# A two-layer hybrid block: the recurrent branch's projection, three pairs inside the recurrent part and one pair behind it

## The chip, the cores and the metric

The kernel runs on one core of a Trainium2 chip. The metric is the device time of one launch in microseconds (us). Three runs of the kernel before took 3108.33, 3111.07 and 3115.43 us; their median is 3111.07 us. About 0.2% (6.2 us) is what a measurement of this kernel can tell from no change.

## The reference, cut to what matters

The program is a block of two layers. Each layer is a feed-forward net, a mixer of three branches (attention, the recurrent branch RWKV7, the state-space branch S5) and a second feed-forward net. Layer 0 works on 512 tokens (256 of the sequence and 256 of the context), layer 1 on the 256 of the sequence.

```python
def gated_merge(z_gate, ya, yr, ys, branch_proj, w_out):
    ga, gr, gs = jnp.split(jax.nn.sigmoid(z_gate), N_BRANCH, axis=-1)
    m = ga * (ya @ branch_proj[0]) + gr * (yr @ branch_proj[1]) + gs * (ys @ branch_proj[2])
    return m @ w_out
```

`yr` is 512 wide: eight heads of 64, that is four pairs of heads of 128. `yr @ branch_proj[1]` is a sum over those four pairs, each of 128 rows of the 512x1024 weight. Ahead of it stands, pair by pair, the branch's `finish`: group normalisation of the scan's output, a bonus term and a gate.

## The kernel before, in words

All activations lie feature-major: a tile has 128 features as partitions and the tokens (512 or 256) as columns. Products of float32 are made as three products of split operands (`mm3`, L153, L154, L155): an operand is a high part (a cast) and a low part (what the cast left out). The split of a weight is a load on SP's queue (L135), a cast on ACT (L136, `wh`) and a subtraction (L137, `wl`) on DVE, or on every second weight on POOL while `k.aside` is set. A weight whose split is made with the priority `AHEAD` stands earlier in the engines' queues than its place in the code. The split of an activation (`split_slot`) is a cast on ACT (L1016) and a subtraction on POOL (L1017).

In the mixer the branches for attention and S5 and the gates' products come first. Then comes what is called the recurrent part here: `conduct` (L980) runs the four pairs' chains of chunks, the last step of each pair being `finish` (L905 to L929), and a filler, the generator `project` (L1645). A stream yields how long it thinks that its step takes, or the name of something that it waits for; `conduct` takes up the first stream whose time has come. In this part PE executes in the order in which the code is written down (`manual_schedule`); the other engines are ordered by a scheduler's priorities. PE's accumulators `acc` have two buffers there, the gates' tiles `sg` two.

`project` makes branch 0 (attention) and branch 2 (S5) with `Merge.branch` (L1573): for each of eight output blocks f of 128 features, a weight of 256 KB, a gate read back from DRAM on ACT's queue (L1584), four times three products into `acc`, and sg = gate * acc on DVE (L1594); for branch 2, m[f] += sg on POOL (L1595).

`finish` of a pair: PE L913 (mean), DVE L917, ACT L918 (square), PE L920 (gate), then a power of the variance (PE L181, DVE L183, POOL L184, ACT L186, PE L190), DVE L923 to L926, and on SP a write of the pair's result to `rwy` in DRAM (L927).

Behind the recurrent part, branch 1 (the recurrent one) is made in the same way: four readbacks of `rwy` (L1570), the splits, eight f with twelve products each, all of this before `m` is split into `mp` (L1690, L1691) and goes through `w_out` in `down` (L381): products L397, L398, L399, the first half of the output's columns streamed weight by weight, the second half kept as eight weights and gone through token tile by token tile.

Of the kernel before, what the change touches and what calls it, by code (L numbers as in the profile page):

```python
# [12 lines left out]
ALU = mybir.AluOpType  # L13
# [11 lines left out]
P = 128  # L25
HIGH = 300
WB, NWA = (3, 3, 3), 2
HELD, NFIRST, AHEAD = 8, 5, 600
# [4 lines left out]
class Ctx:  # L33
# [57 lines left out]
    def late(self, base, tag="late", bufs=12):  # L91
        return self.sp.tile([P, 512], F32, name=self.n(base), tag=tag, bufs=bufs)
# [238 lines left out]
def first_sums(k, w, cols, u, nstream, then):  # L331

    k.more_weights(None, None, None)
    sums = [k.acc() for _ in cols]
    for c, ps in zip(cols, sums):
        k.sum(ps[:, :256], k.columns(w, c, ahead=AHEAD), [(h[:, :256], l[:, :256]) for h, l in zip(*u)])
    if then:
        with k.tc.issue_after(k.mm):
            then()
    return sums  # L340


def other_sums(k, w, cols, u, sums):

    for c, ps in zip(cols, sums):
        k.sum(ps[:, 256:], k.columns(w, c), [(h[:, 256:], l[:, 256:]) for h, l in zip(*u)])
        yield ps
# [665 lines left out]
def split_slot(k, v, n=512):  # L1013
    nc = k.nc
    hi, lo = k.uslot(), k.uslot()
    nc.scalar.copy(hi[:, :n], v[:, :n])  # L1016
    nc.gpsimd.tensor_tensor(lo[:, :n], v[:, :n], hi.bitcast(F32)[:, :n], ALU.subtract)  # L1017
    return hi, lo
# [577 lines left out]
            yield  # L1596


MIX_COLS = [2624 + q * P for q in range(4)] + [i * P for i in (4, 5, 0, 1, 2, 3)]


def mixer(k, first, l, a, u, src, mods, mrows, acst, tab, ctx_out, spill):
    nc, tc = k.nc, k.tc
    ns = 1 + ctx_out
    tok = 256 * ns
# [5 lines left out]
    mg = Merge(k, l, a, gd, tok)  # L1611
    pf = k.pf[l]

    def columns():

        ready = other_sums(k, w_in, MIX_COLS, u, first)
        for i, c in enumerate(MIX_COLS):
            n = tok if c < 512 else 512
# [26 lines left out]
    def project():  # L1645
        gw = s5.glu_weights(a)
        ge = s5.gelu(pf)
        yield 0, 14
        yield from mg.branch(0, mg.load(att.yd), (0, 1.7))
        yield from mg.branch(2, s5.glu(gw, pf, ge, tok), (tok / 140, 0.5))  # L1650

    with ExitStack() as es:
        k.more_weights(es, f"mix{l}", None)
        with ExitStack() as e2:
# [5 lines left out]
            rw = Rwkv(k, l, a, u, w_in, pf, ctx_out)  # L1660
# [21 lines left out]
    with ExitStack() as es:  # L1682
        k.pools(es, f"mixb{l}", 22, (3, 3, 3))
        k.qp = k.pool(es, f"mrg{l}")
        for _ in mg.branch(1, mg.load(rw.yd)):
            pass
        parts = []
        for t in mg.m:
            hi, lo = (k.sp.tile([P, 512], F32R, name=k.n("mp"), tag="mp", bufs=16) for _ in range(2))
            nc.scalar.copy(hi[:, :tok], t[:, :tok])  # L1690
            nc.gpsimd.tensor_tensor(lo[:, :tok], t[:, :tok], hi.bitcast(F32)[:, :tok], ALU.subtract)  # L1691
            parts.append((hi, lo))
        gates_ = [mrows[s, 5 * D:6 * D] for s in range(ns)]
        xt = k.load_x(src)
        r = Residual(k, xt, gates_, a["ln_g"][l, 1], a["ln_b"][l, 1], 1.0)
        md = Modulate(k, mods, 6, 7)

        def close(s, x):
            spill(s, x)
            return md.stream(s, x)  # L1700

        then = down(k, r, [p[0] for p in parts], [p[1] for p in parts], a["w_out"][l], ns, close, 2)
        return md.u, first_sums(k, a["ffn_w_in"][l, 1], FFN_COLS[:NFIRST], md.u, ns, then if ns > 1 else then())
# [5 lines left out]
def full(tc, cst, acst, a, out):  # L1709
    nc = tc.nc  # L1710
    with ExitStack() as ctx:
# [34 lines left out]
        for l in range(DEPTH):  # L1746
            ctx_out = l < DEPTH - 1
            with ExitStack() as es:
# [44 lines left out]
                u = close.md.u  # L1793
                first = first_sums(k, a["w_in"][l], MIX_COLS[:NFIRST], u, 2, then)
            src = [xdram[i] if i < 2 or ctx_out else None for i in range(4)]
            u, first = mixer(k, first, l, a, u, src, mods[l], mrows[l], acst, tabs[l], ctx_out, spill)
            with ExitStack() as es:
                k.pools(es, f"ffb{l}", 46 - 2 * (NF - LATE_H), WMORE)
# [61 lines left out]
```

## Time and profile before

| what | number |
|---|---|
| median of three runs | 3111.07 us |
| the profiled execution | 3109.57 us |
| its span | 3107.8 us |
| PE busy | 2772.4 us, 89% |
| DVE busy | 1595.0 us, 51% |
| ACT busy | 1082.4 us, 35% |
| POOL busy | 746.0 us, 24% |
| layer 0: branch 1's products begin and end | 1233.91 and 1267.09 us |
| layer 1: branch 1's products begin and end | 2838.46 and 2858.11 us |

All times are from the start of the span. A row of a timeline has a start, a duration, the engine (with a q: its queue's own instructions, DMA issues among them), the line of the program, what is written from what, the shape, how many instructions were run together, and in brackets how long the engine was idle before and what released it. The start of one product to the start of the next is what it costs; its duration there is longer, since products overlap.

### The profile page before, as it was taken

The numbers are of one execution on the slowest core, as the hardware profiler recorded it, in microseconds if no ns is written. First come the engines' busy times: TensorE is split into PE (matmuls) and PEld (weight loads), VectorE is DVE, ScalarE is ACT, GpSimd is POOL, SyncE is SP. The second block draws the span as 40 slices with busy tenths as digits, with TensorE's granted clock in tenths as the row PEclk, the third lists the DMA queues.
The fourth block names the chain that finished last, engine by engine and source line by source line (L and its number), as shares of the span: only waits on it lengthen the run. The fifth ranks groups of instructions, "written<-read, shape, count | busy, mean of one in ns | idle before, by whom it ended". The sixth has DMA issues, their size and how long they took to land. (4 is left out here: it accounts for less than half of the span.)

```text
span 3107.8 us, 52359 instructions
## 1 busy us (share of the span) xinstructions
PE 2772.4 (89%) x19886; PEld 2180.3 (70%) x19886; DVE 1595.0 (51%) x3363; ACT 1082.4 (35%) x2140; POOL 746.0 (24%) x940
## 2 busy tenths in 40 slices
PE   4999999899988888989999989999988886687898
PEld 2666788657767665766678877778766776576797
DVE  4655326285445653642232677623549356554555
ACT  3232223344443322242232343322434363333453
POOL 1332103010232213430000335310401232114211
PEclk9999999999998889989999999999989888788899
DMA  7686444934442243568833354453492554254564
GB/s 223 200 258 204 127 164 122 243 91 102 140 106 58 66 114 106 180 202 282 269 110 95 112 137 128 119 160 116 115 222 81 149 134 106 52 110 148 168 185 152
DMA packets 656824, 455.22 MB, mean 146 GB/s; under 512 B 158982, under 2 KB 580980, under 8 KB 648380
## 3 DMA queue, kind: packets, MB, share of 16 engines
q1 hardware_dynamic: 604096, 415.30, 47.1%
q10 hardware_dynamic: 52476, 36.58, 4.3%
q8 instruction: 156, 2.56, 0.3%
q14 instruction: 96, 0.79, 0.1%
HBM read 391.26 MB, written 64.18 MB: 147 GB/s over the span
## 5 line engine op out<-in xcount | busy, mean ns | idle before, releaser
L153 PE MATMUL acc<-u,wh 128*128 128x512 f32 (+1 forms) x2544 | 933.0, 367 | 71.5 <-ACT wh L136 24.0
L155 PE MATMUL acc<-u,wl 128*128 128x512 f32 (+1 forms) x2544 | 916.2, 360 | 27.5 <-DVE wl L137 19.0
L154 PE MATMUL acc<-u,wh 128*128 128x512 f32 (+1 forms) x2544 | 915.6, 360 | 17.4 <-POOL u L289 11.1
L137 DVE TENSOR_TENSOR wl<-wr,wh 128x512 fp32r<-128x512 f32 x720 | 539.8, 758 | 731.0 <-ACT wh L136 712.5
L136 ACT CAST wh<-wr 128x512 fp32r<-128x512 f32 x844 | 513.0, 619 | 1020.3 <-PE acc L154 506.7
L153 PEld LDWEIGHTS acc<-u,wh 128*128 128x128 f32 x2544 | 498.8, 196 | 182.0 <-ACT wh L136 32.6
L155 PEld LDWEIGHTS acc<-u,wl 128*128 128x128 f32 x2544 | 498.9, 196 | 113.7 <-DVE wl L137 27.7
L154 PEld LDWEIGHTS acc<-u,wh 128*128 128x128 f32 x2544 | 498.8, 196 | 95.1 <-POOL u L289 19.5
L137 POOL TENSOR_TENSOR wl<-wr,wh 128x512 fp32r<-128x512 f32 x124 | 170.1, 1378 | 572.2 <-ACT wh L136 549.4
L365 POOL TENSOR_TENSOR hl<-sg,hh 128x512 fp32r<-128x512 f32 (+1 forms) x88 | 108.6, 1234 | 633.6 <-ACT hh L364 586.6
L398 PE MATMUL acc<-wl,hh 128*128 128x512 f32 x616 | 242.1, 393 | 0.0
L399 PE MATMUL acc<-wh,hl 128*128 128x512 f32 x616 | 242.0, 394 | 0.0
L397 PE MATMUL acc<-wh,hh 128*128 128x512 f32 x616 | 241.9, 393 | 0.0
L362 DVE TENSOR_TENSOR sg<-sg,acc 128x512 f32<-128x512 f32 (+1 forms) x88 | 54.5, 620 | 181.4 <-PE acc L155 181.1
L211 PE MATMUL pt<-wa,cond 128*32 128x512 f32 x576 | 101.2, 665 | 40.1 <-DMA wa<-in_w_ada_dram 40.1
L398 PEld LDWEIGHTS acc<-wl,hh 128*128 128x128 f32 x616 | 115.7, 188 | 25.7
L397 PEld LDWEIGHTS acc<-wh,hh 128*128 128x128 f32 x616 | 115.7, 188 | 25.6
L399 PEld LDWEIGHTS acc<-wh,hl 128*128 128x128 f32 x616 | 115.6, 188 | 25.3
L289 POOL TENSOR_TENSOR u<-v,u 128x256 fp32r<-128x256 f32 x88 | 71.5, 828 | 92.8 <-DVE v L288 89.3
L364 ACT CAST hh<-sg 128x512 fp32r<-128x512 f32 (+1 forms) x88 | 49.8, 566 | 102.9 <-DVE sg L362 102.6
L269 ACT ACTIVATE nrm<-x,nb,rstd 128x512 f32<-128x512 f32 x44 | 33.9, 808 | 123.5 <-DVE nb L266 109.5
L211 PEld LDWEIGHTS pt<-wa,cond 128*32 128x32 f32 x576 | 16.2, 112 | 83.5 <-issue 47.3
(346 smaller groups left out, 3715.0 us busy)
## 6 DMA issues: line engine op xcount, KB each, us to landing
wr<-in_ffn_w_in_dram SPq DMA_DIRECT2D x372, 256.0 KB
wa<-in_w_ada_dram SPq DMA_DIRECT2D x64, 1024.0 KB
wr<-in_w_in_dram SPq DMA_DIRECT2D x216, 256.0 KB
wr<-in_ffn_w_out_dram SPq DMA_DIRECT2D x176, 256.0 KB
s5r<-s5tab SPq DMA_DIRECT2D x24, 512.0 KB
wr<-in_branch_proj_dram SPq DMA_DIRECT2D x48, 256.0 KB
s5tab<-s5wo SPq DMA_DIRECT2D x64, 128.0 KB
s5tab<-s5wi SPq DMA_DIRECT2D x64, 128.0 KB
```

The costliest lines, as they stand in the source:

```text
L136: nc.scalar.copy(hi, raw)
L137: (nc.gpsimd if aside else nc.vector).tensor_tensor(lo, raw, hi.bitcast(F32), ALU.subtract)
L153: nc.tensor.matmul(ps, wh, xh, start=first, stop=False)
L154: nc.tensor.matmul(ps, wh, xl, start=False, stop=False)
L155: i = nc.tensor.matmul(ps, wl, xh, start=False, stop=last)
L211: nc.tensor.matmul(ps[32 * ci:32 * ci + 32, :], cond[:, kk, :], w[:, 512 * ci:512 * ci + 512], start=(kk == 0), stop=(kk == 7))
L289: nc.gpsimd.tensor_tensor(lo, v, hi.bitcast(F32), ALU.subtract)
L362: nc.vector.tensor_tensor(sg[:, :ntok], sg[:, :ntok], v[:, :ntok], ALU.mult)
L365: nc.gpsimd.tensor_tensor(h_lo[:, :ntok], sg[:, :ntok], h_hi.bitcast(F32)[:, :ntok], ALU.subtract)
L397: nc.tensor.matmul(ps, hh[f][:, tk], ws[0], start=n == 1, stop=False)
L398: nc.tensor.matmul(ps, hh[f][:, tk], ws[1], start=False, stop=False)
L399: nc.tensor.matmul(ps, hl[f][:, tk], ws[0], start=False, stop=n == nf)
```

## The change

`project` gets a third part, `early`: as soon as `finish0`, `finish1` and `finish2` are done, the three pairs are read back and split, and then for each of the eight f nine products are made (the three pairs' share of the sum). `gated` multiplies with the gate on DVE and adds to m[f], on DVE too. Behind the recurrent part, `late` reads back the fourth pair and makes its three products for each f, with weights of 128x512 (four f to a weight), and calls `gated` again. So each f is gated and added twice, once per part of the sum.

```diff
+    def early(self, yd):
+        for p in range(3):
+            yield f"finish{p}"
+            t = k.q("yu", 3)
+            nc.sync.dma_start(t[:, :tok], yd[p * P:(p + 1) * P, :tok])
+            parts.append(split_slot(k, t, tok))
+            yield 0, 2.5
+        yield 0, 4
+        for f in range(8):
+            ws = k.columns(self.a["branch_proj"][self.l, 1], f * P)
+            ps = k.acc()
+            for kk in range(3):
+                k.mm3(ps[:, :tok], *ws[kk], parts[kk][0][:, :tok], parts[kk][1][:, :tok], kk == 0, kk == 2)
+            self.gated(f, 1, ps)
+            yield 1.5 * tok / 400
+    def late(self, yd):
+        t = k.q("yu", 3)
+        nc.sync.dma_start(t[:, :tok], yd[3 * P:4 * P, :tok])
+        part = split_slot(k, t, tok)
+        w = self.a["branch_proj"][self.l, 1].rearrange("(k p) n -> p k n", p=P)
+        for f in range(8):
+            if f % 4 == 0:
+                hi, lo = k.split_w(w[:, 3:4, f * P:f * P + 512], AHEAD)
+            c = slice(f % 4 * P, f % 4 * P + P)
+            ps = k.acc()
+            k.mm3(ps[:, :tok], hi[:, c], lo[:, c], part[0][:, :tok], part[1][:, :tok], True, True)
+            self.gated(f, 1, ps)
+    def gated(self, f, b, ps):
+        sg = k.q("sg", 2 if k.aside else 3)
+        nc.scalar.dma_start(sg[:, :tok], self.gd[b * 8 + f, :, :tok])
+        nc.vector.tensor_tensor(sg[:, :tok], sg[:, :tok], ps[:, :tok], ALU.mult)
+        nc.vector.tensor_tensor(self.m[f][:, :tok], self.m[f][:, :tok], sg[:, :tok], ALU.add)
...
         yield from mg.branch(2, s5.glu(gw, pf, ge, tok), (tok / 140, 0.5))
+        yield from mg.early(rw.yd)
...
-        for _ in mg.branch(1, mg.load(rw.yd)):
-            pass
+        mg.late(rw.yd)
```

In the diff the new lines of the changed kernel are L1599 to L1639: the readbacks are L1606 (early) and L1622 (late), the gate's transfer L1637, its product L1638, its sum L1639.

Three places show how the instructions move. The first is PE in layer 1, around the last pair's finish (`o` is that pair's output, `pt` a small accumulator). Before:

```order
L892 MATMUL pt_27014<-AR_25420,S_26981 64x64 x2
L913 MATMUL pt_27025<-o_26426,cst 128x256
L920 MATMUL pt_27032<-glo_22580,lg_27027 128x256
L181 MATMUL pt_27034<-cst,o_26426 128x2 x2
L190 MATMUL pt_27043<-cst,X_27041 128x128 x2
L153 MATMUL acc_27101<-u_27071,wh_27094 128x256
L154 MATMUL acc_27101<-u_27072,wh_27094 128x256
L155 MATMUL acc_27101<-u_27071,wl_27095 128x256
```

And now (the first rows left out are the rest of f0 to f5, the second the rest of f6 and f7):

```order
L892 MATMUL pt_27084<-AR_25472,S_27051 64x64 x2
L153 MATMUL acc_27101<-u_26984,wh_27096 128x256
L154 MATMUL acc_27101<-u_26985,wh_27096 128x256
...
L155 MATMUL acc_27201<-u_27042,wl_27197 128x256
L913 MATMUL pt_27215<-o_26478,cst 128x256
L920 MATMUL pt_27222<-glo_22632,lg_27217 128x256
L153 MATMUL acc_27230<-u_26984,wh_27225 128x256
L154 MATMUL acc_27230<-u_26985,wh_27225 128x256
...
L181 MATMUL pt_27264<-cst,o_26478 128x2 x2
L190 MATMUL pt_27273<-cst,X_27271 128x128 x2
L153 MATMUL acc_27311<-u_27301,wh_27306 128x256
```

The last finish's L913 now stands behind 54 products of `early`, and its L181 behind 18 more; the 24 products of `late` follow. In layer 0 PE's order stays finish first, then all 72, then 24.

The second is POOL in layer 0 around the last finish's power (L184; `hr` is the reciprocal root, `u` the low parts of branch 1's input). Before:

```order
L1595 TENSOR_TENSOR m_11280<-m_11280,sg_11717 128x512
L1595 TENSOR_TENSOR m_11322<-m_11322,sg_11749 128x512
L184 TENSOR_TENSOR hr_11772<-hr_11771,mhalf 128x8
L1017 TENSOR_TENSOR u_11807<-yu_11804,u_11806 128x512
L1017 TENSOR_TENSOR u_11813<-yu_11810,u_11812 128x512
L1017 TENSOR_TENSOR u_11819<-yu_11816,u_11818 128x512
```

And now:

```order
L1595 TENSOR_TENSOR m_11280<-m_11280,sg_11717 128x512
L1017 TENSOR_TENSOR u_11780<-yu_11777,u_11779 128x512
L1017 TENSOR_TENSOR u_11796<-yu_11793,u_11795 128x512
L1017 TENSOR_TENSOR u_11802<-yu_11799,u_11801 128x512
L1595 TENSOR_TENSOR m_11322<-m_11322,sg_11749 128x512
L184 TENSOR_TENSOR hr_11772<-hr_11771,mhalf 128x8
L137 TENSOR_TENSOR wl_11867<-wr_11865,wh_11866 128x512
```

The power now stands behind three subtractions for `early`'s input; before, it stood ahead of them.

The third is SP's queue in layer 0 between the write of the last pair's result (L927) and its readback (`yu`). Before:

```order
L927 DMA rwy_5261<-tm_11738 128x512
L1570 DMA yu_11822<-rwy_5261 128x512
L135 DMA wr_11851<-in_branch_proj_dram 128x4x128
L135 DMA wr_11897<-in_branch_proj_dram 128x4x128
L135 DMA wr_11943<-in_branch_proj_dram 128x4x128
L101 DMA x_12044<-xd 128x512
L101 DMA x_12045<-xd 128x512
```

And now (`x` is the residual's input):

```order
L927 DMA rwy_5261<-tm_11738 128x512
L135 DMA wr_11925<-in_branch_proj_dram 128x4x128
L101 DMA x_12096<-xd 128x512
L135 DMA wr_11945<-in_branch_proj_dram 128x4x128
...
L135 DMA wr_12144<-in_w_out_dram 128x512
...
L135 DMA wr_12256<-in_w_out_dram 128x512
L135 DMA wr_12026<-in_branch_proj_dram 128x512
L135 DMA wr_12312<-in_w_out_dram 128x512
L1622 DMA yu_11982<-rwy_5261 128x512
```

The readback stood directly behind the write; now seventeen transfers stand between, the weights of `late` and five of `w_out` among them.

## Rows read from the trace of the kernel before

**Rows 1.** Stretches: us, busy of each engine, granted clock, DMA share, GB/s.

```profile
1233.00:1245.00 12.00, 5.15 (x16) 3.08 (x15) 4.12 (x5) 2.29 (x5) 4.93 (x4) 0.64 0.58 181
1245.00:1267.00 22.00, 21.67 (x86) 17.57 (x87) 12.92 (x14) 7.50 (x13) 13.40 (x11) 0.90 0.84 281
2821.00:2845.00 24.00, 12.79 (x157) 9.95 (x157) 7.55 (x21) 5.75 (x17) 3.87 (x5) 0.68 0.51 153
```

**Rows 2.** Timeline of PE, layer 0: start, duration, engine, line, tiles, [idle before, releaser].

```profile
1226.91 0.40 PE L155 MATMUL acc<-u,wl 128*128 128x512 f32 x1
...
1232.19 2.08 PE L190 MATMUL pt<-cst,X 128*128 128x128 f32 x8 [4.09 <-ACT X L186]
...
1233.91 0.77 PE L153 MATMUL acc<-u,wh 128*128 128x512 f32 x1
...
1237.41 0.40 PE L155 MATMUL acc<-u,wl 128*128 128x512 f32 x1
...
1243.92 0.80 PE L153 MATMUL acc<-u,wh 128*128 128x512 f32 x1 [6.12 <-ACT u L1016]
...
1252.51 0.39 PE L153 MATMUL acc<-u,wh 128*128 128x512 f32 x1
...
1267.09 0.39 PE L397 MATMUL acc<-wh,mp 128*128 128x512 f32 x1
```

**Rows 3.** Timeline of POOL, layer 0, around the last finish.

```profile
1228.17 1.26 POOL L1595 TENSOR_TENSOR m<-m,sg 128x512 f32<-128x512 f32 x1 [2.38 <-DVE sg L1594]
1229.39 2.10 POOL L184 TENSOR_TENSOR hr<-hr,mhalf 128x8 f32<-128x8 f32 x1
1233.09 3.93 POOL L1017 TENSOR_TENSOR u<-yu,u 128x512 fp32r<-128x512 f32 x3 [1.60 <-ACT u L1016]
```

**Rows 4.** Timeline, layer 0: a gate's transfer (ACT's queue) and DVE behind it.

```profile
1220.55 0.33 ACTq L1584 DMA_DIRECT2D sg<-gates  x1
...
1223.34 0.69 DVE L1594 TENSOR_TENSOR sg<-sg,acc 128x512 f32<-128x512 f32 x1 [0.55 <-DMA sg<-gates]
1223.94 0.69 DVE L137 TENSOR_TENSOR wl<-wr,wh 128x512 fp32r<-128x512 f32 x1
...
1228.22 1.76 DVE L137 TENSOR_TENSOR wl<-wr,wh 128x512 fp32r<-128x512 f32 x1
```

**Rows 5.** Timeline, layer 0: SP's queue and ACT, readback of the last pair.

```profile
1240.37 0.32 SPq L1570 DMA_DIRECT2D yu<-rwy  x1
...
1243.25 0.62 ACT L1016 CAST u<-yu 128x512 fp32r<-128x512 f32 x1 [9.20 <-DMA yu<-rwy]
```

**Rows 6.** Timeline of PE, layer 1.

```profile
2829.65 0.69 PE L857 MATMUL pt<-Y,X 64*64 64x64 f32 x8 [2.15 <-ACT Y L850]
...
2832.63 1.19 PE L913 MATMUL pt<-o,cst 128*128 128x256 f32 x2 [0.55 <-DVE o L902]
...
2845.09 0.58 PE L153 MATMUL acc<-u,wh 128*128 128x256 f32 x1 [4.36 <-ACT u L1016]
...
2850.63 0.28 PE L153 MATMUL acc<-u,wh 128*128 128x256 f32 x1
...
2854.18 0.29 PE L153 MATMUL acc<-u,wh 128*128 128x256 f32 x1
...
2858.11 0.39 PE L397 MATMUL acc<-wh,mp 128*128 128x512 f32 x1
...
2873.32 0.73 PE L397 MATMUL acc<-wh,mp 128*128 128x512 f32 x2 [3.97 <-ACT wh L136]
...
2875.95 0.79 PE L398 MATMUL acc<-wl,mp 128*128 128x512 f32 x1 [1.90 <-DVE wl L137]
```

**Rows 7.** Timeline of ACT, layer 1, in the last chain steps.

```profile
2827.54 0.62 ACT L136 CAST wh<-wr 128x512 fp32r<-128x512 f32 x1 [1.56 <-DMA wr<-in_branch_proj_dram]
2828.81 0.62 ACT L136 CAST wh<-wr 128x512 fp32r<-128x512 f32 x1 [0.66 <-DMA wr<-in_branch_proj_dram]
2829.34 0.26 ACT L850 COPY Y<-pt 128x128 f32<-128x128 f32 x1
```

More of the change, by code (lines that the diff above doesn't have):

```diff
@@ L1596, in branch @@
             yield
+    def early(self, yd):
+        k, nc, tok = self.k, self.k.nc, self.tok
+        parts = []
+        for p in range(3):
[13 more added lines that the diff above has]
+    def late(self, yd):
+        k, nc, tok = self.k, self.k.nc, self.tok
+        t = k.q("yu", 3)
[10 more added lines that the diff above has]
+    def gated(self, f, b, ps):
+        k, nc, tok = self.k, self.k.nc, self.tok
+        sg = k.q("sg", 2 if k.aside else 3)
+        nc.scalar.dma_start(sg[:, :tok], self.gd[b * 8 + f, :, :tok])
+        nc.vector.tensor_tensor(sg[:, :tok], sg[:, :tok], ps[:, :tok], ALU.mult)
+        nc.vector.tensor_tensor(self.m[f][:, :tok], self.m[f][:, :tok], sg[:, :tok], ALU.add)
 MIX_COLS = [2624 + q * P for q in range(4)] + [i * P for i in (4, 5, 0, 1, 2, 3)]
```

## The prediction

> **What bounds the kernel now.** I read the page first: TensorE (PE) is busy for 2772.4 of 3107.8 us, so whatever saves time must take away a wait of PE or work of PE. The change takes away no PE work: branch 1 had 8 f x 4 pairs x 3 = 96 products in each layer, and has 72 + 24 = 96. What it can win is a wait. So I went to the stretches around branch 1 [rows 1]: in layer 0 PE is busy for 5.15 of 12 us between 1233 and 1245, at a granted clock of 0.64; in layer 1 for 12.79 of 24 us between 2821 and 2845, at 0.68. Then to PE's timeline there. In layer 0 the reader is to see two waits: 4.09 us ahead of L190, for the power of the last finish, and 6.12 us ahead of the tenth product of branch 1, for the last pair's result, which goes out to DRAM and comes back [rows 2]. In layer 1 the second wait is 4.36 us, and behind the products there are two more in the second half of `w_out`, 3.97 us for a cast and 1.90 us for a subtraction [rows 6].
>
> The profiled execution took 3109.57 us, 1.77 us more than its span, and 1.5 us less than the median of the runs (3111.07). The sum below is made against it, and 1.5 us are added at the end.
>
> **What the change adds.** Per layer: 8 gate transfers, 8 multiplications and 16 additions on DVE in place of 8 additions on POOL, and two weights (loads, casts, subtractions). Laid end to end the 24 new DVE instructions of layer 0 are 24 x 0.69 = 16.6 us by the 0.69 us of L1594 [rows 4]; PE has 96 x 0.231 = 22.2 us of products to hide them (0.231 us is what a product costs at the higher clock, 63 of them from 1252.51 to 1267.09 [rows 2]). As busy time they are covered; as a loop they need not be, see below.
>
> **Layer 0, step by step.** The 72 early products could fill the waits only if they stood ahead of the last finish on PE. The order shows them behind its L190, so the 4.09 us stay.
>
> First, the power is late. POOL now makes three subtractions for early's input ahead of L184. Their slots come free with branch 2's last product, at 1226.91 + 0.40 = 1227.3 [rows 2]; a cast of 0.62 [rows 5], three subtractions in 3.93, one addition to m in 1.26 and the power in 2.10 [rows 3] end at 1235.2. Before, the power ended at 1229.39 + 2.10 = 1231.5. So L190 and what follows it is 3.7 us later: early's products begin at 1233.91 + 3.7 = 1237.6.
>
> Second, the early products. The first nine took 3.7 us before (1233.91 to 1237.41, and one spacing) [rows 2], so f0 ends at 1241.3. Seven more f follow, each 9 x 0.231 = 2.08 us by PE. By the gates: a gate's transfer takes 1223.34 - 1220.55 = 2.79 us from its issue to its multiplication, then come 0.69 for this and 0.69 for the addition, by L137 alone on DVE [rows 4], since the tile is free only then. With two tiles that is 4.17 / 2 = 2.09 us per f: the two limits are level, and early ends at 1241.3 + 7 x 2.09 = 1255.9.
>
> Third, the readback of the last pair. Before it stood directly behind the write on SP. Now the weights of f6 and f7, eight transfers of x, late's two weights and five of `w_out` stand ahead of it, and the last of these waits for a slot that comes free with the split of a `w_out` weight, whose cast waits for the end of early's last products. I take 0.62 for the cast, 1.2 for the subtraction (between 0.69 and 1.76 [rows 4]) and 0.4 for an issue: the readback goes at 1258.1. From issue to the first product with it took 1243.92 - 1240.37 = 3.55 us [rows 2, 5], so late begins at 1261.7. PE waits about 5.8 us there, as it did before for the same data: the wait has moved behind early's products instead of going away. After 6.12 us of idleness the first 24 products took 1252.51 - 1243.92 = 8.59 us [rows 2], so `w_out` begins at 1270.3 instead of 1267.09: +3.2 us. The bounds: if the readback is not held, its data are there at 1243.92 + 3.7 = 1247.6, PE goes on without idleness and 24 x 0.231 = 5.5 us end at 1261.4, -5.7 us; the other end is the slower rival's, +11.
>
> **Layer 1.** Three terms. The chain's last step gets better: its copy Y at 2829.34 stood behind casts that waited for weights (1.56 and 0.66 us) [rows 7], and PE waited 2.15 us for it [rows 6]; now no weight's cast stands between the last chain steps. I take -1.7 (bounds 0 and -2.15). But the last finish now stands behind f0 to f5 on PE: 54 products took 2854.18 - 2845.09 = 9.09 us from the same low clock [rows 6], and f6 and f7 delay its L181 by another 18 x 0.119 = 2.1 us (30 products from 2850.63 to 2854.18). So the last pair's result is late by 9.1 + 2.1 - 1.7 = 9.5 us, and late begins at 2845.09 + 9.5 = 2854.6. Its 24 products take 5.54 us (2850.63 - 2845.09), instead of 87: `w_out` begins at 2860.1, +2.0 us against 2858.11 [rows 6]. Third, nine of the sixteen weights of `w_out` now stand on SP ahead of late, so the two waits in its second half, 3.97 + 1.90 = 5.9 us, should shrink: between nothing and all of it, since PE's own pace frees the slots. I take half, -3.0. Layer 1: -1.0 (bounds +2.0 and -3.9; with the chain's bounds +3.7 and -4.3).
>
> **Sum.** 3.2 - 1.0 = +2.2: 3111.8 for the profiled execution's like, 3113.3 for the median of the runs. I say 3113.
>
> **The rivals.** Faster: the readback is not the last thing. If the transfers ahead of it wait for less than I read from the order, late has its data when early ends; and if the weights of `w_out` flow as freely in layer 1, its two waits go altogether. The sum is -5.7 - 3.9 = -9.6, 3101.5. For it speaks that the first of the transfers ahead of it have nothing on PE to wait for; against it, that the transfer just ahead waits for a slot. It decides from the point at which the readback goes before 1252.4 (1255.9 - 3.55).
>
> Slower: the gate loop. DVE's additions read two tiles, and so does POOL's work beside them. DVE's L137, which reads two tiles as well, took 0.69 us while POOL was idle and 1.76 us beside POOL's addition and power [rows 3, 4], and the DMA engines' share was 0.84 behind 1245 [rows 1], where the early gates will fly beside eight transfers of x. With 1.76 for an addition and 4.0 us for a gate (2.79 x 0.84 / 0.58, an estimate that lets it grow with the share between the two stretches), a pass takes (4.0 + 0.69 + 1.76) / 2 = 3.2 us, early ends 7 x 1.14 = 8.0 us later, layer 0 is at +11.2, and if `w_out` gains nothing in layer 1 that is +2.0: the sum is +13.2, 3124.3. It is slower by more than 0.2% from a pass of 2.7 us on (+4.3 on my sum). The Trainium skill, SBUF — State Buffer, section Who interferes with whom, says that a DVE instruction with two SBUF inputs contends with a GpSimd instruction that reads SBUF. The rows above agree with it; by this rule alone, with each addition at 1.76 and the gate at 2.79, early would end 3.7 us later.
>
> The clock: if the granted clock stays high through the waits, late's 24 products cost 24 x 0.231 = 5.5 us instead of 8.59, and in layer 1 24 x 0.119 = 2.9 instead of 5.54. The sum is 2.2 - 3.1 - 2.6 = -3.5, 3107.6. Against it speak the clocks of 0.64 and 0.68 around waits of this length [rows 1]. The Trainium skill, TensorE: Matmul & The Clock Gate, Part 1, says that the throttled state is the default and that activity releases it; the rows agree.
>
> **How the numbers follow.** My forecast has a chance of 0.43, the faster rival 0.19, the slower 0.28, the clock 0.10. The time to be told from no change is 0.2%, 6.2 us: below 3104.9 is faster, above 3117.3 slower. Forecast and clock fall within it in some nine of ten; the faster rival is nearly all below, the slower in nine of ten above, and the forecast's own upper end adds a little to slower: faster 0.20, same 0.48, slower 0.32. The range leaves out the outer halves of both rivals: 3103 to 3123; my forecast's own range is 3107 to 3118.
>
> **What would show it.** In layer 0 three L1017 ahead of L184 on POOL, and a wait of about 7.8 us (4.09 + 3.7) ahead of L190; early's L1637 gates setting the pace at 2.1 us per f; a wait of about 6 us for ACT's cast of the last pair ahead of late's first product; in layer 1 L913 behind 54 products and shorter waits at L397 and L398. I would be wrong if late's first product follows early's last without a wait, or if PE waits in early for `acc` by more than a microsecond per f.

## The result, and the profile after

The changed kernel took 3131.27 us (median of six runs, 3125.10 to 3139.31), the kernel before 3109.70 in the same series (3102.43 to 3115.43): a ratio of 1.0076, interval 1.0057 to 1.0096. It is slower by 21.6 us where I had forecast +2.2, and lies above the upper end of my range. The profiled execution's span is 3128.9 us, 21.1 more than before.

Runs of one and the same kernel lie some 20 us apart, so I count inside one trace, between three marks: the last chain step of the last pair (the last L892 on PE), `w_out`'s first product (L397), and the last wait ahead of `w_out`'s second half.

| us from the last L892 | layer 0: `w_out` | layer 0: last wait | layer 1: `w_out` | layer 1: last wait |
|---|---|---|---|---|
| before | 51.8 | 80.0 | 26.7 | 44.6 |
| changed | 67.0 | 95.6 | 33.5 | 48.6 |

The marks that [rows 2] and [rows 6] do not show, first those of the kernel before, then the first one of the changed kernel:

```profile
1215.34 0.45 PE L892 MATMUL pt<-AR,S 64*64 64x64 f32 x8
1295.33 0.80 PE L398 MATMUL acc<-wl,mp 128*128 128x512 f32 x1 [2.10 <-DVE wl L137]
2831.39 0.69 PE L892 MATMUL pt<-AR,S 64*64 64x64 f32 x8
```

```profile
1213.17 0.45 PE L892 MATMUL pt<-AR,S 64*64 64x64 f32 x8
```

Layer 0 lost 15.6 us, layer 1 lost 4.0: 19.6 of the 21.1. The first view is that of stretches, with the columns of [rows 1]:

```profile
1245.00:1267.00 22.00, 10.77 (x37) 7.44 (x36) 10.61 (x16) 2.91 (x5) 1.87 (x2) 0.82 0.98 329
2821.00:2849.00 28.00, 22.86 (x310) 19.76 (x310) 13.72 (x33) 8.48 (x25) 13.70 (x15) 0.89 0.37 109
```

In layer 0 the same 22 us in which PE was busy for 21.67 before now have PE busy for 10.77, and the DMA share went from 0.84 to 0.98, from 281 to 329 GB/s. In layer 1 the stretch that had the wait is well filled now; its loss must lie behind it. The timeline of PE in layer 0, against [rows 2]:

```profile
1233.14 2.07 PE L190 MATMUL pt<-cst,X 128*128 128x128 f32 x8 [7.16 <-ACT X L186]
1234.87 0.77 PE L153 MATMUL acc<-u,wh 128*128 128x512 f32 x1
...
1246.04 0.47 PE L153 MATMUL acc<-u,wh 128*128 128x512 f32 x1 [0.98 <-DVE sg L1638]
...
1251.41 0.47 PE L153 MATMUL acc<-u,wh 128*128 128x512 f32 x1 [3.05 <-DVE sg L1638]
...
1257.94 0.47 PE L153 MATMUL acc<-u,wh 128*128 128x512 f32 x1 [0.45 <-DVE sg L1638]
...
1259.86 0.39 PE L155 MATMUL acc<-u,wl 128*128 128x512 f32 x1
1271.29 0.80 PE L153 MATMUL acc<-u,wh 128*128 128x512 f32 x1 [11.04 <-ACT u L1016]
...
1280.20 0.48 PE L397 MATMUL acc<-wh,mp 128*128 128x512 f32 x1 [0.30 <-DVE sg L1638]
...
1306.13 0.50 PE L397 MATMUL acc<-wh,mp 128*128 128x512 f32 x1 [1.51 <-ACT wh L136]
...
1308.74 0.79 PE L398 MATMUL acc<-wl,mp 128*128 128x512 f32 x1 [2.11 <-DVE wl L137]
```

The wait ahead of L190 grew from 4.09 to 7.16. Early's products begin at 1234.87 and, with three waits for the gating DVE, end 25.4 us later. Then comes the wait that I had put at 5.8 us: 11.04. The power's delay is plain in POOL's timeline, against [rows 3]: the three subtractions now stand ahead of L184.

```profile
1225.46 4.16 POOL L1017 TENSOR_TENSOR u<-yu,u 128x512 fp32r<-128x512 f32 x3 [1.62 <-ACT u L1016]
1229.58 1.26 POOL L1595 TENSOR_TENSOR m<-m,sg 128x512 f32<-128x512 f32 x1
1230.80 1.64 POOL L184 TENSOR_TENSOR hr<-hr,mhalf 128x8 f32<-128x8 f32 x1
```

What paces early stands in the timelines of POOL, DVE and ACT's queue, against [rows 4] (L1637 issues a gate, L1638 multiplies with it, L1639 adds to `m`):

```profile
1239.46 1.28 POOL L137 TENSOR_TENSOR wl<-wr,wh 128x512 fp32r<-128x512 f32 x1 [7.02 <-ACT wh L136]
1239.76 1.53 DVE L1639 TENSOR_TENSOR m<-m,sg 128x512 f32<-128x512 f32 x1
1241.33 0.33 ACTq L1637 DMA_DIRECT2D sg<-gates  x1
1243.13 0.33 ACTq L1637 DMA_DIRECT2D sg<-gates  x1
1245.21 0.69 DVE L1638 TENSOR_TENSOR sg<-sg,acc 128x512 f32<-128x512 f32 x1 [2.11 <-DMA sg<-gates]
1245.93 0.69 DVE L1639 TENSOR_TENSOR m<-m,sg 128x512 f32<-128x512 f32 x1
...
1250.58 0.69 DVE L1638 TENSOR_TENSOR sg<-sg,acc 128x512 f32<-128x512 f32 x1 [3.95 <-DMA sg<-gates]
...
1255.27 0.33 ACTq L1637 DMA_DIRECT2D sg<-gates  x1
...
1261.30 0.69 DVE L1638 TENSOR_TENSOR sg<-sg,acc 128x512 f32<-128x512 f32 x1 [2.77 <-DMA sg<-gates]
```

Early's first two gates were fetched ahead of it. From issue to multiplication the first gate fetched inside the loop, f2's, took 3.9 us, the next 7.4 (1243.13 to 1250.58), f6's 6.0, where [rows 4] had 2.79. DVE waits for gates, and PE for the accumulators that they hold. Last in layer 0, the readback, against [rows 5], with DVE's last subtraction ahead of it:

```profile
1255.86 8.55 SPq L135 DMA_DIRECT2D wr<-in_w_out_dram  x2
...
1264.58 0.68 DVE L137 TENSOR_TENSOR wl<-wr,wh 128x512 fp32r<-128x512 f32 x1
...
1265.66 0.42 SPq L1622 DMA_DIRECT2D yu<-rwy  x1
...
1270.61 0.62 ACT L1016 CAST u<-yu 128x512 fp32r<-128x512 f32 x1 [1.67 <-DMA yu<-rwy]
```

SP was held until weight slots came free; their subtractions stand on DVE behind the late gates. The readback went at 1265.66 and took 4.95 us to the cast, before 2.88.

Layer 1: PE's timeline, against [rows 6], then the readback on SP and ACT:

```profile
2847.08 0.69 PE L857 MATMUL pt<-Y,X 64*64 64x64 f32 x8 [0.42 <-ACT Y L850]
...
2848.82 0.69 PE L892 MATMUL pt<-AR,S 64*64 64x64 f32 x8
2849.45 0.58 PE L153 MATMUL acc<-u,wh 128*128 128x256 f32 x1
...
2859.51 0.59 PE L913 MATMUL pt<-o,cst 128*128 128x256 f32 x2
...
2865.01 0.71 PE L190 MATMUL pt<-cst,X 128*128 128x128 f32 x4 [1.78 <-ACT X L186]
...
2875.74 0.58 PE L153 MATMUL acc<-u,wh 128*128 128x256 f32 x1 [10.02 <-ACT u L1016]
...
2882.33 0.47 PE L397 MATMUL acc<-wh,mp 128*128 128x512 f32 x1 [1.05 <-DVE sg L1638]
...
2896.04 0.73 PE L397 MATMUL acc<-wh,mp 128*128 128x512 f32 x2 [2.36 <-ACT wh L136]
...
2897.43 0.69 PE L398 MATMUL acc<-wl,mp 128*128 128x512 f32 x1 [0.66 <-DVE wl L137]
```

```profile
2867.98 0.33 SPq L927 DMA_DIRECT2D rwy<-tm  x1
...
2869.85 0.33 SPq L1622 DMA_DIRECT2D yu<-rwy  x1
...
2875.28 0.40 ACT L1016 CAST u<-yu 128x256 fp32r<-128x256 f32 x1 [1.36 <-DMA yu<-rwy]
```

The products that fill the chain's end stand ahead of the last finish: from L892 to L190 it is 16.2 us now, 6.2 before. Then the data of the last pair make their way to DRAM and back, and PE waits 10.02 us for them, with only 24 products left to do. The stretch of that wait shows the transfers crowded there too, the loads of `w_out` and `x` that were issued beside the readback:

```profile
2865.00:2880.00 15.00, 4.75 (x21) 4.27 (x22) 6.12 (x14) 2.26 (x4) 1.99 (x2) 0.56 0.92 303
```

### The profile page after: what moved, and what is told of

It reads as the page before. It is cut to its first block, busy times and chain, and to the rows that moved or that the text cites. A ratio compares the mean times of both kernels' runs of the same rounds, so it can differ in the third digit from the quotient of the medians.

```text
span 3128.9 us, 52443 instructions
## 1 busy us (share of the span) xinstructions
PE 2774.3 (89%) x19886; PEld 2182.1 (70%) x19886; DVE 1613.6 (52%) x3405; ACT 1084.2 (35%) x2144; POOL 741.8 (24%) x934
## 5 line engine op out<-in xcount | busy, mean ns | idle before, releaser
L155 PE MATMUL acc<-u,wl 128*128 128x512 f32 (+1 forms) x2544 | 918.1, 361 | 27.8 <-DVE wl L137 19.6
L154 PE MATMUL acc<-u,wh 128*128 128x512 f32 (+1 forms) x2544 | 917.5, 361 | 16.2 <-POOL u L289 10.5
L137 DVE TENSOR_TENSOR wl<-wr,wh 128x512 fp32r<-128x512 f32 x714 | 529.5, 750 | 720.9 <-ACT wh L136 702.9
L154 PEld LDWEIGHTS acc<-u,wh 128*128 128x128 f32 x2544 | 500.8, 197 | 92.6 <-POOL u L289 18.7
L137 POOL TENSOR_TENSOR wl<-wr,wh 128x512 fp32r<-128x512 f32 x134 | 184.6, 1383 | 620.5 <-ACT wh L136 601.0
L397 PE MATMUL acc<-wh,hh 128*128 128x512 f32 x616 | 241.9, 393 | 0.0
L397 PEld LDWEIGHTS acc<-wh,hh 128*128 128x128 f32 x616 | 115.7, 188 | 25.5
L361 ACT ACTIVATE sg<-acc 128x512 f32<-128x512 f32 (+1 forms) x88 | 47.5, 540 | 77.6 <-PE acc L155 70.7
```

The costliest lines, as they stand in the source:

```text
L137: (nc.gpsimd if aside else nc.vector).tensor_tensor(lo, raw, hi.bitcast(F32), ALU.subtract)
L154: nc.tensor.matmul(ps, wh, xl, start=False, stop=False)
L155: i = nc.tensor.matmul(ps, wl, xh, start=False, stop=last)
L397: nc.tensor.matmul(ps, hh[f][:, tk], ws[0], start=n == 1, stop=False)
```

## The experiments

The theory after the result: the loss is three waits in series. **Gates**: early's gates are slow because they share the DMA engines with `x` and weights. **Readback**: the last pair comes back late because its transfer stands behind things that wait for the gates. **Finish**: in layer 1 the last pair's finish is late. The rivals: the power alone, `x` alone, the loop's depth (two gate tiles), and what became a theory only later, the **second gating**: each f is gated a second time in `late`, which I had taken as free. Letters in the quoted expectations are the names that the theories had when these were written. Every ratio is against the kernel before on the same chip, with its 95% interval. "Local" is the change against before to the last wait, layer 0 and layer 1, in the one trace of that kernel.

| kernel | ratio | local, us |
|---|---|---|
| e1_layer0_only | 1.0046 (1.0029 to 1.0064) | +14.4, -0.1 |
| e2_layer1_only | 1.0032 (1.0016 to 1.0049) | +1.1, +4.9 |
| e4_three_gate_tiles | 1.0098 (1.0077 to 1.0120) | +12.7, +6.0 |
| e6_one_gate | 1.0087 (1.0063 to 1.0110) | +7.3, +5.4 |
| e10_gates_ahead | 1.0043 (1.0027 to 1.0059) | +7.6, +8.0 |
| e5_x_behind | 1.0069 (1.0043 to 1.0095) | +15.4, +6.8 |
| e3_readback_in_part | 1.0085 (1.0061 to 1.0109) | +13.0, +12.5 |
| e7_one_gate_readback | 1.0072 (1.0044 to 1.0100) | +2.8, +10.3 |
| f3_l0_power_first | 1.0035 (1.0019 to 1.0051) | +11.8, -2.1 |
| e11_layer0_all_three | 0.9993 (0.9975 to 1.0010) | +4.9, -0.7 |
| f4_l0_four | 0.9995 (0.9978 to 1.0011) | +5.1, -1.8 |
| e8_l1_finish_first | 1.0023 (1.0006 to 1.0040) | +0.8, +11.3 |
| f1_l1_readback_weights | 1.0053 (1.0038 to 1.0069) | +0.4, +10.8 |
| f2_l1_and_gates | 1.0032 (1.0015 to 1.0048) | +0.1, +10.0 |
| f7_l1_no_late_gate | one run, 3114.09 against 3113.88 | +0.4, +1.9 |
| e9_split_order | 1.0002 (0.9984 to 1.0020) | -3.0, -0.5 |
| e12_split_x | 0.9985 (0.9965 to 1.0005) | -4.3, +0.5 |
| f6_split_x_half | 1.0006 (0.9990 to 1.0021) | -3.6, -0.7 |

A layer that a kernel leaves as it was shows what one trace can tell: +0.1 to +1.1 us in layer 0, -0.1 to -2.1 in layer 1. In e4, e6 and e7 the space for one more tile was taken from the readbacks (`yu`, two tiles for three). All three are 6 to 9 us longer than the changed kernel in each layer ahead of the marks (from the second finish to the third), so their totals carry some 14 to 16 us that their local numbers don't; no run has this edit alone. For the other rows the local sum times 1/3112 lies in the ratio's interval or within 0.0004 of it.

**Which layer.** e1 makes the change in layer 0 alone, e2 in layer 1 alone:

```diff
-        yield from mg.early(rw.yd)
+        if ctx_out:                      # e2: if not ctx_out
+            yield from mg.early(rw.yd)
...
-        mg.late(rw.yd)
+        if ctx_out:
+            mg.late(rw.yd)
+        else:
+            for _ in mg.branch(1, mg.load(rw.yd)): pass
```

> The change in layer 0 alone; layer 1 is as before. The two traces differ by about 13.5 us at the first product of w_out in layer 0 and by 21.1 us at the end. Theory A (layer 0's readback and gates carry the loss): 13 to 15 us slower than before, about two thirds of the 21.6. Rival (the loss is made in layer 1 by the finish that stands behind 54 products, and layer 0's shift is made good later): within 5 us of before.

> The change in layer 1 alone. Theory A: 6 to 8 us slower than before, so that this run and the one with layer 0 alone add up to the whole. Rival (the finish behind 54 products carries the loss): 15 us slower or more. My forecast's own term for layer 1 was -1.

Measured +0.46% and +0.32%, together the whole 0.76%. Each layer loses by itself. That layer 0 loses more is read from the marks (+14.4 and +4.9); the two intervals overlap.

**The gates of layer 0.** e4 gives early, and the two branches ahead of it, a third gate tile; e6 loads one gate for all f of early (it leaves out seven of eight gate transfers and multiplies every f with that one gate); e10 puts early's gates into eight tiles that the S5 branch has done with, so that they can be loaded ahead.

```diff
-        sg = k.q("sg", 2 if k.aside else 3)
+        sg = k.q("sg", 3)                                  # e4, and yu 3 -> 2
+        sg = k.q(tag, 4) if tag else k.q("sg", ...)        # e10
-            self.gated(f, 1, ps)
+            self.gated(f, 1, ps, self.g1)                  # e6, and yu 3 -> 2
+            self.gated(f, 1, ps, ("gw", "ge")[f % 2])      # e10
```

> The whole change, with three tiles for the gates in the recurrent part instead of two (and two for the branches' inputs instead of three, to make room). In the changed kernel the gates of layer 0's early took 3.9 to 7.4 us from issue to multiplication. Theory B (two tiles pace early): early's 25.4 us in layer 0 fall to about 19, so the kernel gets 4 to 7 us faster than the changed one. Rival (transfers share the DMA engines, so more in flight take longer each): early stays at 24 us or more, and the time stays within 2 us.

> The whole change, with work left out: early reads one gate for all eight f (seven of eight transfers per layer are gone) and keeps its DVE work. Theory C (the second reading of the gates is the cost): early in layer 0 is bound by PE and DVE, 15 to 18 us instead of 25.4, but late still waits for its readback, so 6 to 10 us faster than the changed kernel. Rival (DVE's additions or POOL beside them pace early): early stays over 21 us.

> The whole change, with early's gates in the eight tiles that branch 2's gelu has done with, so that all eight are in flight ahead of early; nothing else is made smaller for it (the run with three tiles cut the branches' input tiles, and lost 7 to 9 us in the part ahead of it). Theory B (two tiles pace early): in layer 0 early falls from 25.4 us to 18 to 20, and from the last chain step to w_out's second wait it takes 88 to 91 us instead of 95.6 (80.0 before). Rival (the DMA engines pace it): 94 us or more.

Layer 0's local loss falls from 15.6 to 12.7 with a deeper loop, to 7.3 without the transfers and to 7.6 with the gates ahead. Not all of this is the gates: the wait ahead of L190 is 5.94, 4.36 and 5.59 us in these three, 7.16 in the changed kernel. What the gates cost is read from early itself. It took 25.4 us in the changed kernel (24.5 and 24.4 in e1 and e3, which leave it as it is), 22.5 in e4, 18.7 in e6 and 18.7 in e10, whose first and last early products are:

```profile
1239.26 0.77 PE L153 MATMUL acc<-u,wh 128*128 128x512 f32 x1
...
1257.52 0.39 PE L155 MATMUL acc<-u,wl 128*128 128x512 f32 x1
```

So 6.7 us are the gates in flight, by two kernels that take them away in different ways, and the depth of the loop is the smaller part (2.8 us). In e10 the share of the DMA engines between 1245 and 1271 is 0.88 at 303 GB/s. In layer 1 e10 lost 4.0 us against the changed kernel; I did not follow that up.

**The transfers of x.** e5 holds `x` back until the last weight of `late`:

```diff
+        with tc.issue_after(dm):      # the last weight's load of late
             xt = k.load_x(src)
```

> The whole change, but the eight transfers of x (256 KB each) stand on SP behind the weights of late and the readback, not ahead of them. Theory C (early's gates are slow because they share the DMA engines with x, weights and broadcast rows, at a share of 0.95 in the changed kernel): early's gates in layer 0 come back to 3 to 4 us and early takes 19 to 21 us instead of 25.4; 4 to 8 us faster than the changed kernel (3131). Rival (the gates are slow by themselves, as two tiles and a chain of waits on ACT's queue): gates still take 4 to 7 us, early 24 us or more, within 2 us of the changed kernel.

Early took 22.4 us there instead of 25.4, with a gate in 2.9 to 5.1 us at a DMA share of 0.68 (1250 to 1268): `x` beside the gates is some 3 of their 6.7 us, and neither the theory (19 to 21 us) nor its rival (24 or more) had it. From L190 to `w_out` it took 42.6 us instead of 47.1, but then `w_out` itself waited (1.82 us at one product), and at the last wait 95.4 against 95.6: nothing. The transfers only trade places; what is taken out of early's way is missing behind it.

**The readback.** e3 takes the last pair's tile inside the recurrent part, at the end of `early`, and issues its readback and split with priority; e7 adds it to e6 (and leaves out the same).

```diff
+        yield "finish3"
+        t = k.q("yu", 3)
+        with k.tc.high_priority(offset=AHEAD):
+            nc.sync.dma_start(t[:, :tok], yd[3 * P:4 * P, :tok])
+            self.part = split_slot(k, t, tok)
...
     def late(self, yd):
-        t = k.q("yu", 3)
-        nc.sync.dma_start(t[:, :tok], yd[3 * P:4 * P, :tok])
-        part = split_slot(k, t, tok)
+        part = self.part
```

> The whole change, but the last pair's readback and split are written at the end of early, into a tile of the recurrent part's own pool, with priority; it then stands one or two transfers behind its write on SP instead of 17. Theory A (the readback is held by its place, since its tile lies in memory that early's gates still use): late's first product follows early's last without the 11 us wait in layer 0 and with 6 us of 10 gone in layer 1; 12 to 16 us faster than the changed kernel. Rival (the DMA engines are the limit around 1245 to 1271, at a share of 0.95): the transfer itself is as late, under 5 us faster.

> One gate for early as in the run beside it (work left out) and the readback of the last pair in the recurrent part. With the readback alone, late waited 5.87 us for an accumulator that early's last gate held, in place of 11 us for the data. Theory D (two waits in parallel, each enough to hold late): with both taken away w_out begins 34 to 37 us behind L190 in layer 0 instead of 47, and the kernel is 12 to 18 us faster than the changed one. Rival (a third thing holds late, as its weights did in layer 1): under 10 us faster.

In e3 the data were back 20 us before they were needed (issued at 1245.71, cast at 1250.04), and layer 0 gained 2.6 us only. PE's timeline there (L1641 is the gates' multiplication in this kernel) shows who came in its place:

```profile
1269.74 0.77 PE L153 MATMUL acc<-u,wh 128*128 128x512 f32 x1 [5.87 <-DVE sg L1641]
...
1275.51 0.50 PE L153 MATMUL acc<-u,wh 128*128 128x512 f32 x1 [1.06 <-ACT wh L136]
```

The accumulator of late's first product was still held by early's last gate, and late's second weight came late. With one gate the same edit (e7 against e6) gains 4.5 us. So the 11.04 us were two waits on top of one another; taking the one away uncovers the other. In layer 1 e3 lost 8.5 us against the changed kernel, with a wait of 4.09 us for late's second weight. e3 changes the readback's place on SP and the pool of its tile at once; which of the two held it was not told apart.

**The power, and all of it together.** f3 (layer 0 alone) puts early's three splits behind the last finish's power; e11 has this with e3's and e10's edits; f4 also lets late's weights start the round of weight slots anew.

```diff
+            with k.tc.issue_after(k.pow):          # f3, e11, f4
                 parts.append(split_slot(k, t, tok))
...
             if f % 4 == 0:
+                k.wi = 0                            # f4
```

> The change in layer 0 alone, with POOL's power of the last finish ahead of early's three subtractions and nothing else. By my first term PE's wait ahead of L190 falls from 7.16 to 4.1 us. Theory G (the delay goes through to the end): 91 to 92 us from the last chain step to w_out's second wait, against 94.4. Rival (the gates and the readback are later than it in any case): 94 us or more.

> The change in layer 0 alone, with its three waits taken away: gates ahead, the last pair's readback in the recurrent part, and POOL's power ahead of the three subtractions. Theory D (these three are the whole of layer 0's loss of 15.6 us): from the last chain step to w_out's second wait 76 to 81 us (80.0 before, 95.6 with the change), and the kernel within 4 us of before. Rival (the doubled reading of the gates costs by itself, 2 MB more in a stretch at a DMA share of 0.84): 85 us or more, 5 to 8 us slower than before.

> The change in layer 0 alone with four things taken away: power first, gates ahead, readback in the recurrent part (these three gave 84.9 us against 94.4 with the change in layer 0 and 80.0 before), and late's second weight, for which PE then waited 3.4 + 0.6 us. Theory D: 79 to 82 us; what is left over 80 is late's own second gating. If the second gating were free it would be 76 or less, and the kernel faster than before.

The power first is worth 2.6 us (14.4 to 11.8), and reaches the end. All of it brings layer 0 from +14.4 to +4.9, and in total back to a time that can't be told from that of before (0.9993 and 0.9995). Theory D had 76 to 81 us and 79 to 82 to the last wait; 84.9 and 85.1 are misses. f4 removed the weight's wait of e11 (3.42 us) and nothing was gained; this row of PE (f4) says why (L1643 is the multiplication):

```profile
1262.80 0.80 PE L153 MATMUL acc<-u,wh 128*128 128x512 f32 x1 [6.48 <-DVE sg L1643]
```

Late's second gating holds the accumulators. That had no term in my sum. For layer 0 this row is the evidence; no run there leaves the second gating out.

**Layer 1.** e8 (layer 1 alone) lets early wait for the last finish, so that the order is that of layer 0. f1 is e3's edit and f4's round of slots in layer 1 alone; f2 adds e10's gates; f7 is f2 with late's products added to `m` without the gate (late's eight gates and multiplications are left out).

```diff
+        if tok < 512: yield "finish3"     # e8, ahead of early's loop over f
         yield 0, 4
...
+        if tag is None:                   # f7, in gated: late's products
+            nc.vector.tensor_tensor(self.m[f][:, :tok], self.m[f][:, :tok], ps[:, :tok], ALU.add)
+            return
```

> The change in layer 1 alone, with all 72 early products behind the last finish instead of 54 ahead of it. Theory E (the finish behind 54 products makes layer 1's loss): from the last chain step to w_out's second wait 42 to 45 us (44.6 before, 49.5 with the change in layer 1 alone). Rival (the gates and the readback's place make it, as in layer 0): 48 us or more.

> The change in layer 1 alone, with the last pair's readback in the recurrent part and late's two weights in the part's own slots, so that neither stands behind x or w_out. From the last chain step to w_out's second wait: 44.6 us before, 49.5 with the change in layer 1, 57.1 with the readback alone moved (late's second weight was then the wait, 4.1 us). Theory F (the readback's place and the second weight's place hold late): 44 to 47 us, the layer's loss gone. Rival (the last pair's result comes too late in any case, being behind f0 to f7): 49 us or more.

> As the run beside it, and early's gates ahead in eight tiles. Theory F: f0 to f5 then cost PE 9 us or less and the finish comes earlier: 1 to 3 us below the run beside it. Rival (gates are no limit in layer 1, where a gate tile is half as big): equal within 1 us.

> The change in layer 1 alone with readback, weights and early's gates as in the run f2 (54.6 us from the last chain step to w_out's second wait), and with work left out: late's products are added without their gate, so its eight gate transfers and multiplications are gone. Theory H (what stays in layer 1 is late's second gating, 4.4 + 1.5 us of PE's waits): 48 to 50 us. Rival (the finish behind f0 to f5 is all of it): 53 us or more.

e8 made layer 1 worse locally (+11.3, with a wait of 11.17 us for the readback), though its time (1.0023) can't be told from e2's (1.0032): the finish's place is not the whole story, since the readback then waits behind other work on SP as in layer 0. In f1 and f2 the readback's wait fell from 10.02 to 6.54 and 6.19, and the gates' came up: 4.28 + 1.81 and 4.35 + 1.45. Both kernels were some 5 us worse at the last wait than e2 (+10.8 and +10.0 against +4.9), so theory F missed; f2 is 0.8 us below f1, as its rival had it. The rows of f2, of ACT's queue, DVE and PE (L1641 issues the gate, L1642 multiplies):

```profile
2852.67 3.39 ACTq L1641 DMA_DIRECT2D sg<-gates  x3
...
2860.78 0.42 DVE L1642 TENSOR_TENSOR sg<-sg,acc 128x256 f32<-128x256 f32 x1 [12.41 <-DMA sg<-gates]
...
2861.26 0.58 PE L153 MATMUL acc<-u,wh 128*128 128x256 f32 x1 [4.35 <-DVE sg L1642]
```

Late's first gate is issued only behind the cast of the last pair and lands 8 us later. Without the second gating, f7, the local loss falls from 10.0 to 1.9: the second gating costs some 7 to 8 us of layer 1 once the readback is early (6.8 of the 8.1 lie behind L190). In f7 the last finish still stands behind 54 products of `early`, so its place alone is not what layer 1 loses by. What is left there is the weights, in f7's row of PE:

```profile
2865.67 1.22 PE L397 MATMUL acc<-wh,mp 128*128 128x512 f32 x2 [3.31 <-ACT wh L136]
```

**A version that might win.** If the second gating is the price, the products should be made in two parts without it: e9 takes the kernel before and only reorders branch 1: the 27 products of pairs 0 to 2 for three f, then the last pair's readback and split, then their last products and one gating, then f3 to f7 as before. e12 moves the loads of `x` behind `w_out`'s streamed weights as well; f6 moves half of `x`, in layer 0.

```diff
-        for _ in mg.branch(1, mg.load(rw.yd)): pass
+        mg.behind(rw.yd)
+    def behind(self, yd):
+        ...
+        for f in range(3):
+            k.wi = 0                       # the round of weight slots anew
+            weights(f)
+            for kk in range(3): products(f, kk)
+        parts.append(split_slot(k, next(y), tok))
+        for f in range(3):
+            products(f, 3)
+            close(f)                       # the gate, once per f
+        for f in range(3, 8): ...          # twelve products and close(f)
```

> The kernel before, with another order behind the recurrent part: for the first three f the products of three pairs (27) stand ahead of the last pair's readback and their products, each f is gated once. It fills the wait of 6.12 us (layer 0) and 4.36 us (layer 1) without a second gating: 18 products more ahead of the wait, 18 x 0.231 = 4.2 us and 18 x 0.213 = 3.8 us, so 6 to 10 us faster than before. If the DMA engines and not PE's order set when w_out begins, within 3 us of before.

> The kernel before with the split order (three f's products for three pairs ahead of the last pair's readback; 77.0 us instead of 80.0 in layer 0 and 44.1 instead of 44.6 in layer 1), and the transfers of x behind the streamed weights of w_out on SP. In that run w_out waited 0.7 + 0.9 us in layer 0 and 1.7 + 1.6 us in layer 1 for its first weight. If x stood in its way: 74 to 76 and 40 to 42 us, 5 to 9 us faster than before in all. If the weights wait for slots: no different from the split order alone, within 4 us of before.

> The kernel before with the split order (77.0 us in layer 0 instead of 80.0, 44.1 in layer 1 instead of 44.6), and in layer 0 the context's half of x (four transfers of eight) behind the streamed weights of w_out. With all of x behind them the first wait for w_out's weights went and 5 + 2 us came back in its second half. If half of x is enough: 73 to 76 us in layer 0, and 3 to 7 us faster than before in all. If the transfers only trade places again: 77 us or more, no change.

PE in layer 0 of e9, against [rows 2]:

```profile
1243.73 0.60 PE L153 MATMUL acc<-u,wh 128*128 128x512 f32 x1 [1.86 <-ACT u L1016]
...
1289.47 0.50 PE L397 MATMUL acc<-wh,mp 128*128 128x512 f32 x1 [1.52 <-ACT wh L136]
...
1292.09 0.79 PE L398 MATMUL acc<-wl,mp 128*128 128x512 f32 x1 [2.11 <-DVE wl L137]
```

The wait of 6.12 fell to 1.86, in layer 1 that of 4.36 to 2.22. Locally 3.0 and 0.5 us are gained; in time that cannot be told from nothing (1.0002). In e12 `w_out` begins without a wait for weights, and its second half waits instead (lines are six higher there):

```profile
1257.04 0.50 PE L403 MATMUL acc<-wh,mp 128*128 128x512 f32 x1 [0.34 <-DVE sg L1625]
...
1282.30 0.67 PE L403 MATMUL acc<-wh,mp 128*128 128x512 f32 x1 [4.95 <-ACT wh L142]
```

From L190 to the last wait layer 0 took 58.8 us in e12, 59.5 in f6, 60.1 in e9 and 63.1 before; as one trace of each, with an interval that reaches over 1, I do not call e12 faster. It stays open whether it is.

## Why the prediction was wrong

- **The power**: +3.7 forecast, 12.63 against 9.53 us from L913 to L190 measured, +3.1. Right, and f3 shows that it reaches the end.
- **Early's products**: this step failed: "With two tiles that is 4.17 / 2 = 2.09 us per f: the two limits are level". Early took 25.4 us, not 18.3: +7.1. The loop was the right mechanism; its transfer was mis-sized. I took 2.79 us from a stretch with a DMA share of 0.63 (1220.5 to 1223.4) [rows 4], and the gates fetched inside early took 3.9 to 7.4 us in a stretch whose share was already 0.84 [rows 1] and went to 0.98. Of the 7.1 us some 4.5 are PE's three waits, and 1.8 are the products of f5 and f6 behind the wait of 3.05 us: the granted clock was 0.54 there (1252.2 to 1255.9), near the lower of its two levels (1.2 GHz), and products followed one another by 0.43 us and more instead of 0.23. e6 and e10 confirm the cause: 18.7 us for early, near the 18.3 forecast. e10 reads as many gates as the changed kernel, so it is not their bytes alone but that the loop waits for them.
- **The readback**: held by what I named, a weight's slot behind early's last work, but it went 5.4 us behind early's end (1260.25 to 1265.66), where I had 2.2, and the way to PE was 5.6 us, not 3.55. The wait was 11.04, not 5.8: +5.2. Some 3.2 of it follow from the step before, since the slot's subtraction stands on DVE behind the gates; 2.1 are the slower transfer.
- **Late's products in layer 0**: 8.9 us against 8.59. Right: as in [rows 2] behind a wait, the granted clock was at its lower level (0.50 between 1271.3 and 1276.2), and the first products followed one another by 0.43 us, at the higher level by 0.23. Together 3.2 + 7.1 + 5.2 + 0.3 - 0.6 (the power) = 15.2 us, which is what 67.0 - 51.8 gives.
- **Layer 1's finish**: +11.2 forecast against L892 (9.1 + 2.1), +10.0 measured. Right.
- **Layer 1's readback**: I priced no change; from SP's issue to the cast it took 5.43 us at a DMA share of 0.92, before 2.15 (+3.3). A term that was missing.
- **Layer 1's chain**: -1.7 forecast. PE's wait of 2.15 us is gone (0.42 now), but from the second to the third finish it took 97.4 us against 94.8, and kernels whose layer 1 is as before took from 92.4 (f4) to 97.3 (e1). No net gain is seen; +1.7.
- **24 products instead of 87**: -7.5 forecast, -6.4 measured, the difference being the wait of 1.05 for a gate ahead of L397.
- **`w_out`'s second half**: -3.0 forecast, -2.7 measured (15.1 against 17.8 from its first product to the last wait).
- **The rivals**: the slower one had the mechanism, the gates beside `x` at a high DMA share, at 8.0 for the 7.1 measured. That these are so near is luck: its gate of 4.0 us was too short, and its addition of 1.76 too long, since all but one of early's took 0.69. Its reading of the 0.69 us of DVE's L137 in [rows 4] was wrong too: POOL was not idle, its addition began at 1224.11, within that instruction, and took 1.68 us. It ended at 3124.3, too low, because it, too, left the readback at its old length. Neither sum has the second gating, which in the changed kernel shows as small waits of `w_out` (0.30, 0.59 and 0.58 us in layer 0, 1.05 in layer 1) and grows only once the readback is early. The clock rival and the faster one are refuted by the 11.04 us wait and the 8.9 us behind it.

Of my signs to look for, "PE waits in early for `acc` by more than a microsecond per f" came true once (3.05 us); the wait ahead of L190 was 7.16, forecast 7.8.

Layer 0's and layer 1's excess over the forecast, 12.4 + 5.0 = 17.4 us, is most of the 19.4 between +2.2 and +21.6; the remaining 2 us lie between the marks of one trace and the medians, and were not followed.

## What to carry to other kernels

Splitting a sum that is multiplied by something read from memory doubles those reads: price the second reading, and every accumulator that it holds, before the wait that the split should fill. A loop that goes through a transfer has to be priced by the transfer's time in the stretch in which it will run, with its own bytes added, not by the same transfer in a quiet stretch. Where a wait for the last operand is to be filled, reorder the products ahead of one common gating (e9's wait fell from 6.12 to 1.86 us), and look at the transfers behind: of the 4.3 us 3.0 were left at the last wait of one trace, and nothing that the time of a launch can show.

## What the runs showed of the hardware

From issue to use, a gate of 256 KB took 2.79 us at a share of the DMA engines of 0.63 (before, 1220.5 to 1223.4), and in the changed kernel 3.9 us at 0.76 (1241 to 1245.3) and 7.4 us at 0.97 (1243 to 1250.6); the readback, of the same size, went from 2.88 us at 0.64 (1240 to 1244) to 4.95 us at 0.86 (1265 to 1271). In layer 1 the last readback, half as large, took 5.43 us at a share of 0.92, before 2.15 (there the share was 0.51 and 162 GB/s between 2835 and 2850). In these four comparisons the time grew with the share, by a factor between 1.4 and 2.7; no run varied the share alone.

An addition on DVE with two tiles as inputs took 0.69 us alone and 1.53 us beside POOL's subtraction of 1.28 us, at 1239.76. The Trainium skill, SBUF — State Buffer, section Who interferes with whom, says that a DVE instruction with two SBUF inputs contends with a GpSimd instruction that reads SBUF; the trace agrees, and also shows how seldom the two met: once in early's eight additions.
